# One value product per head from a sum of two masked matrices, and four adaLN sections of the second layer as row sums on VectorE

## The chip, the core and the metric

The kernel runs on one core of a Trainium2 chip. Its engines work in parallel, each through its own queue of instructions in order: PE (TensorE, matrix products), DVE (VectorE, elementwise work), ACT (ScalarE, activations and copies), POOL (GpSimd, here memsets and a few small loads) and SP (SyncE, which issues nearly all loads). The metric is the device time of one execution in microseconds (us), lower is better.

## What is computed

The reference is a two-layer transformer block. There are 256 latent and 256 context tokens of width 1024. Each layer has modulated RMSNorm, one input projection, three parallel head groups (A: differential attention, B: windowed attention, C: bidirectional gated linear attention), an output projection and a feed-forward part: a dense SwiGLU of width 2816 in the first layer, a top-2 of 8 experts SwiGLU of width 3584 in the second. Cut to the two places that the change touches:

```python
for layer in range(DEPTH):
    mod_l = (silu_c @ ada_w[layer] + ada_b[layer])[:, None, :]      # 6 sections of 1024
    mod_c = (silu_cc @ ada_w[layer] + ada_b[layer])[None, None, :]
    sh1_l, sc1_l, g1_l, sh2_l, sc2_l, g2_l = jnp.split(mod_l, 6, axis=-1)
    ...
    h_l = rms_norm(xl, norm1_g[layer]) * (1.0 + sc1_l) + sh1_l

# group C, forward and again on the flipped sequence, the two results added
att = jnp.where(causal, jnp.einsum('nbhcd,nbhsd->nbhcs', q_dec, k_inv), 0.0)
o_intra = jnp.einsum('nbhcs,nbhse->nbhce', att, vc)
```

The adaLN product has only two rows, the SiLU of the condition of the latent tokens and that of the context tokens, against a matrix of 1024 x 6144 per layer (25 MB in fp32). Everything is fp32; large products are made of three passes over high and low parts of the operands (hhi, hlo, whi, wlo).

## The kernel before

The whole kernel is planned before it is written: `add` registers each operation with its engine, an estimated time, what it waits for, a rank and the rings (buffers in rotation) that it takes and gives back. A list scheduler then starts, on each engine, the ready operation of lowest rank, and the instructions go out in that order. So a change of one operation can reorder others around it.

In time the stages of the profiled execution are: start and input projections of the first layer to about 190 us, its attention to 340, the dense FFN from about 352 to 715, the second layer's norm, projection and mixing (latent tokens only as queries) to about 950, and the experts to the end.

**The adaLN product.** `ada` makes `nb` blocks of 128 columns of one layer. It loads the columns of `ada_w` in two halves of four 128-row blocks through SP's queue, into a ring of large buffers. For each half it issues four products, L442, in which the two condition rows (padded to 32) are the small operand and the weights stream through as `nb * 128` columns; each product has its own 32 output columns of the array. ACT copies the result (L219, tile adar), PE transposes it (L452, tile adat), and DVE adds the four partial rows and the bias (L456, L457). In the FFN, `fill` is a list of such calls that `ffn` hands out, two after each chunk: two blocks of three for the last sections of the first layer, and then blocks 0 to 31 of the second layer, which are its first four sections, as ten calls of three blocks and one of two. The second layer's other two sections come later, in its mixing.

**The dense FFN.** Two halves of 1408 columns, each in chunks of at most 512. For each chunk the weights come in 1 MB loads; ACT makes the high part (whi, L219) and DVE the low part (wlo, L385); PE runs the three passes L645, L646 and L647 over 512 tokens. ACT takes the SiLU of the gate (fsg, L1651), DVE multiplies (L1658) and forms fhl.

**Group C.** `outC` makes one tile of 128 tokens (two chunks of 64) with four heads. For each head PE forms the products of keys and queries for both directions (paC, L1070); DVE copies those that the mask admits into one of two buffers of two 128x128 matrices, which hold zeros elsewhere (att, L1078); PE then multiplies each of the two matrices with the same values and adds both into poC (L1074). The first layer has 4 such tiles, the second 2, so 24 heads in all.

Of the kernel before, what the change touches and what calls it, by code (L numbers as in the profile page):

```python
# [11 lines left out]
F32 = mybir.dt.float32  # L12
# [10 lines left out]
KD = 8  # L23
# [9 lines left out]
def _const_arrays():  # L33
# [55 lines left out]
class Plan:  # L89
# [83 lines left out]
def trunk(ctx: ExitStack, tc: tile.TileContext, A, out, dbg=None):  # L173
# [101 lines left out]
            between()  # L275
        newton()

    plan = Plan(big=2, sm=4, hi=2, lo=2, raw=2, sp=2, work=10, long=24, mixC=2, b16=2, units=5, oC=2)
    add = plan.add


# [184 lines left out]
        return have  # L466

    mod = {}

    def amul(l, sec, g, nm):  # L470

# [186 lines left out]
    wmaskb = pc.tile([128, 2, 128], BF)  # L658
    bonesT = C("bones")
    att_bufs = []  # L660
    for i in range(2):
# [146 lines left out]

    wg, wu, wd = A["ffn_w_gate"][0], A["ffn_w_up"][0], A["ffn_w_down"][0]
    FILL = 5000  # L810
    EARLY = 32

    def mixing(l, base, t, tiles, wC, started=None):

# [235 lines left out]
        def outC(i, have, rank):  # L1050
            w = {}
            prev = None
            for pr in range(2):
# [9 lines left out]
                for hh in range(2):  # L1063
                    h = 2 * pr + hh

                    def products_(pr=pr, hh=hh, h=h):
                        r = slice(64 * hh, 64 * hh + 48)
                        w["pa", h] = P1((128, 2, 128), nm="paC")
                        for dr in range(2):
                            mm(w["pa", h][:, dr, :], G["ki", i, pr][r, dr, :], G["qd", i, pr][r, dr, :], start=True, stop=True)  # L1070

                    def values(hh=hh, h=h):
                        for dr in range(2):
                            mm(w["po"][:, 96 * h:96 * h + 96], att_bufs[hh][:, dr, :], T["vC", i][:, 96 * h:96 * h + 96],  # L1074
                               start=False, stop=hh == 1 and dr == 1)

                    a = add("PE", 0.44, products_, [x, *done["qk", i, pr]], rank, ["sm"])
                    a = add("DVE", 0.36, lambda hh=hh, h=h: nc.vector.copy_predicated(att_bufs[hh], mask, w["pa", h]),  # L1078
                            [a, turn.get(hh)], rank, (), ["sm"])
                    prev = turn[hh] = add("PE", 0.4, values, [a, prev, done["vC", i]], rank, (),  # L1080
                                          ["work"] + (["sp"] if pr == 1 else []) if hh == 1 else ())

            def copied_():
# [409 lines left out]
        for b in range(EARLY if last else 16, 48 if last else 42, 2):  # L1493
# [96 lines left out]
    def ffn(base, t, tiles, first_rank):  # L1590
# [3 lines left out]
                kk = 4 * hk + k  # L1594
                mm3(at(m), w.w[0][:, k, ms], w.w[1][:, k, ms], t["hi"][:, kk, :], t["lo"][:, kk, :], kk == 0, kk == KD - 1)

        fill = [(0, b, min(3, 48 - b)) for b in range(42, 48, 3)] + [(1, b, min(3, EARLY - b)) for b in range(0, EARLY, 3)]
        read = []
        sums = [[], []]
        silu = None  # L1600
        for g in range(2):
# [3 lines left out]
            for ci, (c0, cn) in enumerate(((0, 512), (512, 512), (1024, 384))):  # L1605
# [959 lines left out]
```

## Time and profile before

| | |
|---|---|
| three runs | 1921.57, 1925.91, 1927.15 us, median 1925.91 |
| the profiled execution | 1931.52 us, span in the trace 1929.7 us, mean granted clock of PE 0.99 |
| PE busy | 1880.7 us, 97% of the span |
| DVE busy | 1368.1 us, 71% |
| ACT busy | 1135.9 us, 59% |
| POOL busy | 38.9 us, 2% |
| moved by DMA | 474 MB, mean 246 GB/s |
| chain that ended last | PE 86%, DVE 6%, DMA 4%, ACT 3%; L442 of `ada` alone 2% |

The profile is one execution; its own time is the one against which a sum can be made, and it lies 5.6 us above the median of the three runs. The share of busy time is an average over stages, and a busy PE says little of how well it is fed, since the ends of matmuls are modelled; what a matmul costs is better read from the distance of two starts. In the rows below, a tile's name is the program's, an arrow points from inputs to output, and the bracket behind an instruction gives the idle time just before it and what ended it.

### The profile page before, as it was taken

How to read it: one execution, taken by the hardware profiler on the slowest of the kernel's cores; microseconds unless marked ns; L12 is line 12 of the kernel's file. 1: busy time of each engine (PE TensorE's matmuls, PEld its weight loads, DVE VectorE, ACT ScalarE, POOL GpSimd, SP SyncE). 2: the span in 40 equal slices, each digit the busy share in tenths (PEclk: the TensorE clock that was granted, in tenths of full speed). 3: DMA queues.
4: the chain of work that ended last, by engine and by line, in shares of the span. 5: the costliest groups of instructions: out<-in, count | busy, mean ns of one | idle time of the engine just before them, and what ended most of it. 6: DMA issues, size and time to landing. Idle time of an engine off the chain costs nothing.

```text
span 1929.7 us, 27430 instructions
## 1 busy us (share of the span) xinstructions
PE 1880.7 (97%) x10129; PEld 1511.6 (78%) x10129; DVE 1368.1 (71%) x2269; ACT 1135.9 (59%) x1906; POOL 38.9 (2%) x44
## 2 busy tenths in 40 slices
PE   7999999999999999999999999999999999999997
PEld 4888678877787799887888767888886688888765
DVE  5564887433333345758799786999988789999787
ACT  4443774323132325448677676777777777777676
POOL 1000200000000000011000000000000000000000
PEclk9999999999999999999999998999999999999999
DMA  9313532445434422347789898999999999999992
GB/s 295 109 55 101 183 105 82 139 135 185 164 120 137 153 74 88 93 141 245 258 316 359 343 374 341 368 362 381 355 352 368 397 360 360 380 366 363 356 366 104
DMA packets 178318, 474.38 MB, mean 246 GB/s; under 512 B 13193, under 2 KB 74337, under 8 KB 164481
## 3 DMA queue, kind: packets, MB, share of 16 engines
q1 hardware_dynamic: 177792, 472.37, 68.0%
q8 instruction: 82, 1.34, 0.3%
q0 software_dynamic: 384, 0.19, 0.1%
q14 instruction: 60, 0.48, 0.1%
HBM read 471.47 MB, written 1.05 MB: 245 GB/s over the span
## 4 chain that ended last, share of the span: by engine, by line
PE 86%; DVE 6%; DMA 4%; ACT 3%; issue 1%; SPq 0%; DVEq 0%; ACTq 0%
PE py L2311 12%; PE up L2229 12%; PE gate L2229 12%; PE acc L645 9%; PE acc L647 8%; PE acc L646 8%; DVE mlo L1885 2%; PE adap L442 2%; PE acc L855 2%; DMA idle<-in_ada_w 2%; PE acc L857 2%; PE acc L856 2%; PE py L2309 1%; PE pT L1241 1%; PE mtp L2288 1%; ACT mhi L219 1%
## 5 line engine op out<-in xcount | busy, mean ns | idle before, releaser
L1885 DVE TENSOR_TENSOR mlo<-early,mhi 128x1024 fp32r<-128x1024 f32 (+1 forms) x250 | 278.6, 1160 | 25.1 <-ACT mhi L219 23.5
L219 ACT ACTIVATE mhi<-early 128x1024 fp32r<-128x1024 f32 (+1 forms) x252 | 237.7, 996 | 43.7 <-PE py L2311 18.7
L385 DVE TENSOR_TENSOR wlo<-raw,whi 128x512 fp32r<-128x512 f32 (+4 forms) x292 | 150.4, 564 | 157.8 <-ACT whi L219 157.1
L219 ACT ACTIVATE whi<-raw 128x512 fp32r<-128x512 f32 (+4 forms) x292 | 134.9, 525 | 181.8 <-PE acc L646 147.0
L645 PE MATMUL acc<-hhi,whi 128*128 128x512 f32 (+1 forms) x576 | 217.4, 377 | 2.9 <-DVE rC L885 1.9
L1885 DVE TENSOR_TENSOR mlo<-more,mhi 128x1024 fp32r<-128x1024 f32 (+1 forms) x176 | 202.2, 1196 | 25.4 <-ACT mhi L219 23.5
L646 PE MATMUL acc<-hlo,whi 128*128 128x512 f32 (+1 forms) x576 | 210.6, 366 | 2.4 <-DVE hlo L579 2.4
L647 PE MATMUL acc<-hhi,wlo 128*128 128x512 f32 (+1 forms) x576 | 210.6, 366 | 0.5 <-DVE wlo L385 0.5
L2311 PE MATMUL py<-mhi,hid 128*128 128x512 f32 x696 | 193.7, 405 | 6.9 <-ACT mhi L219 3.7
L219 ACT ACTIVATE mhi<-more 128x1024 fp32r<-128x1024 f32 (+1 forms) x176 | 171.8, 1031 | 26.6 <-PE up L2229 12.9
L2311 PEld LDWEIGHTS py<-mhi,hid 128*128 128x128 f32 x696 | 131.5, 192 | 42.6 <-ACT mhi L219 9.7
L1885 DVE TENSOR_TENSOR mlo<-mraw,mhi 128x1024 fp32r<-128x1024 f32 (+1 forms) x116 | 134.5, 1202 | 16.6 <-ACT mhi L219 16.5
L1885 DVE TENSOR_TENSOR mlo<-spare,mhi 128x1024 fp32r<-128x1024 f32 (+1 forms) x114 | 129.7, 1183 | 10.8 <-ACT mhi L219 10.6
L645 PEld LDWEIGHTS acc<-hhi,whi 128*128 128x128 f32 x576 | 108.7, 189 | 35.2 <-issue 11.2
L2311 PE MATMUL py<-mlo,hid 128*128 128x512 f32 x416 | 122.4, 407 | 2.5 <-DVE mlo L1885 2.5
L219 ACT ACTIVATE mhi<-mraw 128x1024 fp32r<-128x1024 f32 (+1 forms) x116 | 114.2, 1036 | 18.1 <-PE py L2311 9.2
L646 PEld LDWEIGHTS acc<-hlo,whi 128*128 128x128 f32 x576 | 108.9, 189 | 19.2 <-DVE hlo L579 3.4
L647 PEld LDWEIGHTS acc<-hhi,wlo 128*128 128x128 f32 x576 | 108.7, 189 | 18.7 <-DVE wlo L385 0.9
L219 ACT ACTIVATE mhi<-spare 128x1024 fp32r<-128x1024 f32 (+1 forms) x114 | 110.2, 1020 | 14.4 <-PE py L2311 9.6
L2311 PEld LDWEIGHTS py<-mlo,hid 128*128 128x128 f32 x416 | 79.3, 193 | 26.7 <-DVE mlo L1885 11.0
L2229 PE MATMUL gate<-mlo,xh 128*128 128x512 f32 x280 | 78.4, 402 | 0.0
L2229 PE MATMUL gate<-mhi,xh 128*128 128x512 f32 x280 | 76.0, 394 | 0.0
(443 smaller groups left out, 3693.3 us busy)
## 6 DMA issues: line engine op xcount, KB each, us to landing
early<-in_moe_w_gate SPq DMA_DIRECT2D x42, 1024.0 KB, 7.4
early<-in_moe_w_down SPq DMA_DIRECT2D x41, 1024.0 KB, 6.5
more<-in_moe_w_gate SPq DMA_DIRECT2D x38, 1024.0 KB, 7.0
early<-in_moe_w_up SPq DMA_DIRECT2D x37, 1024.0 KB, 7.0
mraw<-in_moe_w_up SPq DMA_DIRECT2D x25, 1024.0 KB, 6.6
spare<-in_moe_w_down SPq DMA_DIRECT2D x25, 1024.0 KB, 6.8
more<-in_moe_w_up SPq DMA_DIRECT2D x25, 1024.0 KB, 7.3
more<-in_moe_w_down SPq DMA_DIRECT2D x25, 1024.0 KB, 5.7
```

Of the source, the lines that this page charges most:

```text
L219: act(o, i, AF.Copy)
L385: tt(l_, v, h, op=OP.subtract)
L442: mm(w["pm"][32 * g:32 * g + 32, :n], sil[:, 4 * i + g, :], w["raw"][4 * i + g], start=i == 0, stop=i == 1, tile_position=(0, 32 * g))
L645: mm(o, lh, rh, start=start, stop=False)
L646: mm(o, lh, rl, start=False, stop=False)
L647: mm(o, ll, rh, start=False, stop=stop)
L855: mm(p, t["hi"][:, kk, s], w.w[0][:, k, :], start=kk == 0, stop=False)
L856: mm(p, t["hi"][:, kk, s], w.w[1][:, k, :], start=False, stop=False)
L857: mm(p, t["lo"][:, kk, s], w.w[0][:, k, :], start=False, stop=kk == KD - 1)
L1885: tt(l, w, h, op=OP.subtract)
L2229: mm(outs[q], x[a](kk), w[b][:, j, :], start=i + kk == 0, stop=i == len(x) and kk == KD - 1)
L2311: mm(outs[q], v[a][:, kk % 4, :], w[b][:, j, :], start=first and i + kk == 0, stop=i == len(v) and kk + 1 == nk)
```

## The change

Two things are changed.

In group C, DVE adds the two masked 128x128 matrices of a head (atts, one more TENSOR_TENSOR behind each L1078), and PE multiplies the sum with the values: one product instead of two.

The second layer's sections 0 to 3 are taken out of `fill`. A new function `ada_rows` makes each of them in two halves of 512 columns. The weights of a half come as eight loads of 128x512 (256 KB) on the Pool queue, into a ring of three buffers (adw). DVE multiplies each with the two conditions, one value per partition, and sums up: per half 2 TENSOR_SCALAR and 14 SCALAR_TENSOR_TENSOR of 128x512. Then, for each condition, DVE transposes 32x32 blocks and reduces (2 of each per half). One PE product per section with a constant 128x128 matrix (`four`) adds the four groups of 32 rows and lays the sum out, and DVE adds the bias in four small pieces. So there are 64 loads, 16 TENSOR_SCALAR, 112 SCALAR_TENSOR_TENSOR, 16 transposes, 16 reductions, 4 products and 16 small additions. All of it but the last two steps has the rank `base + 9000`, behind the FFN's own work. The bytes of `ada_w` are the same as before; 22 loads of SP's queue are gone. The constant adds 64 KB to an early load.

```diff
+    c["four"] = p[:, None] % 32 == p[None, :] % 32
...
+    def ada_rows(l, sec, rank, after):
...
+        for j in range(2):
+            c0 = sec * 1024 + j * 512
+            for k in range(KD):
+                def load(k=k, c0=c0):
+                    w["w"] = k2.tile([128, 1, 512], F32, name="adw", tag="adw", bufs=3)
+                    w[k] = w["w"]
+                    nc.gpsimd.dma_start(out=w[k], in_=A["ada_w"][l, k * 128:k * 128 + 128, c0:c0 + 512].rearrange("(k p) f -> p k f", p=128))
+
+                after = [add("PoolDMA", 0.75, load, after, rank, ["adw"])]
+                for i in range(1):
+                    for v in range(2):
+                        def summed(k=k, i=i, v=v):
...
+                            o, x, s = w["acc"][:, v], w[k][:, i], sil[:, k + i, v:v + 1]
+                            if k + i == 0:
+                                ts(o, x, s, None, op0=OP.mult)
+                            else:
+                                stt(o, x, s, o, op0=OP.mult, op1=OP.add)
...
+            for v in range(2):
+                def grouped(v=v, j=j):
...
+                    nc.vector.transpose(t, w["acc"][:, v])
+                    nc.vector.tensor_reduce(w["r"][:, v, 4 * j:4 * j + 4].rearrange("p m q -> p (m q)"),
+                                            t.rearrange("p (b i) -> p b i", i=32), axis=AX.X, op=OP.add)
...
+        def over_groups():
+            w["p"] = P1((128, 2, 8, 4), nm="adap")
+            mm(w["p"].rearrange("p v m q -> p (v m q)"), C("four"), w["r"].rearrange("p v m q -> p (v m q)"), start=True, stop=True)
...
-    EARLY = 32
+    ROWS = 4
...
+                    def masked(hh=hh, h=h):
+                        nc.vector.copy_predicated(att_bufs[hh], mask, w["pa", h])
+                        tt(att_sums[hh], att_bufs[hh][:, 0, :], att_bufs[hh][:, 1, :], op=OP.add)
+
                     def values(hh=hh, h=h):
-                        for dr in range(2):
-                            mm(w["po"][:, 96 * h:96 * h + 96], att_bufs[hh][:, dr, :], T["vC", i][:, 96 * h:96 * h + 96],
-                               start=False, stop=hh == 1 and dr == 1)
+                        mm(w["po"][:, 96 * h:96 * h + 96], att_sums[hh], T["vC", i][:, 96 * h:96 * h + 96], start=False, stop=hh == 1)
...
-        fill = [(0, b, min(3, 48 - b)) for b in range(42, 48, 3)] + [(1, b, min(3, EARLY - b)) for b in range(0, EARLY, 3)]
+        fill = [(0, b, min(3, 48 - b)) for b in range(42, 48, 3)]
...
+                if rows_ is None:
+                    rows_ = read[:1]
+                    for sec in range(ROWS):
+                        rows_ = ada_rows(1, sec, base + 9000 + sec, rows_)
```

On PE, in the FFN, one removed block of `ada` stands between the three passes of the FFN like this (before):

```order
L647 MATMUL acc_4366<-hhi,wlo 128x512
L442 MATMUL adap<-idle,sil 32x384 x4
L645 MATMUL acc<-hhi,whi 128x512
...
L647 MATMUL acc<-hhi,wlo 128x512
L442 MATMUL adap<-idle,sil 32x384 x4
L645 MATMUL acc_4366<-hhi,whi 128x512
...
L647 MATMUL acc_4366<-hhi,wlo 128x512
L452 MATMUL adat<-cst,adar 128x128 x3
L645 MATMUL acc_4366<-hhi,whi 128x512
```

After, PE has for a whole section this one product there (the passes' lines are 59 higher):

```order
L706 MATMUL acc<-hhi,wlo 128x512
L515 MATMUL adap<-adsum,cst_80 128x64
L704 MATMUL acc_4301<-hhi,whi 128x512
L705 MATMUL acc_4301<-hlo,whi 128x512
L706 MATMUL acc_4301<-hhi,wlo 128x512
```

The three matmuls that were between the parts of a block now follow each other without them.

On DVE, at the FFN's start, the low parts of the first weights and the first products stand like this (before):

```order
L385 TENSOR_TENSOR wlo<-raw,whi 128x512 x12
L1658 TENSOR_TENSOR fsg<-fsg,acc 128x512
L385 TENSOR_TENSOR fhl<-fsg,fhh 128x512
L1658 TENSOR_TENSOR fsg<-fsg,acc 128x512
L385 TENSOR_TENSOR fhl<-fsg,fhh 128x512
```

And after:

```order
L386 TENSOR_TENSOR wlo<-raw,whi 128x512 x8
L496 TENSOR_SCALAR adacc<-adw,sil 128x512 x2
L498 SCALAR_TENSOR_TENSOR adacc<-adw,sil,adacc 128x512 x9
L386 TENSOR_TENSOR wlo<-raw,whi 128x512 x4
L1720 TENSOR_TENSOR fsg<-fsg,acc 128x512
L498 SCALAR_TENSOR_TENSOR adacc<-adw,sil,adacc 128x512
L386 TENSOR_TENSOR fhl<-fsg,fhh 128x512
L1720 TENSOR_TENSOR fsg<-fsg,acc 128x512
```

Eleven of the new sums, which use five and a half loads, stand ahead of the low parts of the next weights, and single ones between the FFN's own operations.

On PE, in group C of the second layer, the products with the values (poC from vC) and their neighbours stand like this before, where att_95 and att_97 are the two buffers:

```order
L1074 MATMUL poC<-vC_6926,att_95 128x96 x2
L1074 MATMUL poC<-vC_6926,att_97 128x96 x2
L1058 MATMUL poC<-spC,qkC 128x192 x2
L1070 MATMUL paC<-qkC 128x128 x4
L645 MATMUL acc_7150<-hhi,whi 128x256
```

And after, where atts_95 and atts_96 are the sums:

```order
L1137 MATMUL poC<-vC_7038,atts_95 128x96
L1130 MATMUL paC<-qkC 128x128 x2
L1137 MATMUL poC<-vC_7038,atts_96 128x96
L1118 MATMUL poC<-spC,qkC 128x192 x2
L1130 MATMUL paC<-qkC 128x128 x2
L704 MATMUL acc_7262<-hhi,whi 128x256
```

Each head has one product with the values instead of two, and the key-query products of the next heads have come apart around them.

## Rows read from the trace of the kernel before

**Rows 1.** Windows: a stretch, its length, busy us per engine, clock, DMA
```profile
core 0: us, PE busy (x) PEld busy (x) DVE busy (x) ACT busy (x) POOL busy (x), PEclk, DMA share, GB/s
358.00:615.00 257.00, 256.16 (x1216) 197.30 (x1216) 82.83 (x159) 71.83 (x134) 0.00 (x0) 1.00 0.46 152
...
1100.00:1500.00 400.00, 394.08 (x1770) 313.36 (x1769) 344.73 (x338) 295.22 (x349) 0.00 (x0) 0.99 0.96 364
```

**Rows 2.** Timeline of PE in the FFN without `ada`: start, us, instruction, twelve passes apart
```profile
423.33 0.39 PE L647 MATMUL acc<-hhi,wlo 128*128 128x512 f32 x1
...
426.05 0.39 PE L647 MATMUL acc<-hhi,wlo 128*128 128x512 f32 x1
```

**Rows 3.** Timeline of PE around one block whose halves stand apart
```profile
480.13 0.39 PE L647 MATMUL acc<-fhh,wlo 128*128 128x512 f32 x1
480.45 0.85 PE L442 MATMUL adap<-idle,sil 128*32 128x384 f32 x8
...
483.87 0.39 PE L647 MATMUL acc<-fhh,wlo 128*128 128x512 f32 x1
...
487.60 0.39 PE L647 MATMUL acc<-fhh,wlo 128*128 128x512 f32 x1
487.83 0.49 PE L452 MATMUL adat<-cst,adar 128*128 128x128 f32 x3
...
490.70 0.39 PE L647 MATMUL acc<-fhh,wlo 128*128 128x512 f32 x1
```

**Rows 4.** Timeline of PE around a block whose halves stand together
```profile
498.86 0.39 PE L647 MATMUL acc<-fhh,wlo 128*128 128x512 f32 x1
499.18 1.50 PE L442 MATMUL adap<-idle,sil 128*32 128x384 f32 x16
...
503.27 0.39 PE L647 MATMUL acc<-fhh,wlo 128*128 128x512 f32 x1
```

**Rows 5.** Waits of PE in the FFN, 360 to 720: total us, times, longest
```profile
PE acc L645 <- ACT fsg L1651: 0.7, 2, 0.4
```

**Rows 6.** Timeline of PE, group C of the first layer: the products with the values
```profile
106.72 1.11 PE L1074 MATMUL poC<-vC,att 128*128 128x96 f32 x8
107.67 0.52 PE L1058 MATMUL poC<-spC,qkC 128*128 128x192 f32 x2
```

**Rows 7.** Group C of the second layer: timelines of DVE and PE, and the window
```profile
804.08 0.77 DVE L1078 COPY_PREDICATED att<-cst,paC 128x256 f32<-128x256 uint32 x2
...
804.58 1.13 PE L1074 MATMUL poC<-vC,att 128*128 128x96 f32 x8 [0.44 <-DVE att L1078]
...
801.00:816.00 15.00, 14.56 (x114) 12.49 (x113) 9.43 (x28) 4.35 (x13) 0.00 (x0) 1.00 0.39 124
```

**Rows 8.** DVE by line and shape: count, busy us, mean ns, idle before
```profile
L1281 DVE SCALAR_TENSOR_TENSOR unit<-unit,rcA 128x512 f32<-128x512 f32 x16 | 12.1, 755 | 0.2
L1323 DVE TENSOR_SCALAR unit<-unit,smx 128x512 f32<-128x512 f32 x24 | 10.8, 482 | 0.1
...
L385 DVE TENSOR_TENSOR wlo<-raw,whi 128x128 fp32r<-128x128 f32 x16 | 4.6, 285 | 0.0
L1236 DVE TENSOR_REDUCE mx<-sB 128x2 f32<-128x512 f32 x6 | 4.1, 688 | 1.2 <-PE sB L1221 1.0
```

**Rows 9.** Timeline of DVE at the FFN's start
```profile
354.19 4.91 DVE L385 TENSOR_TENSOR wlo<-raw,whi 128x512 fp32r<-128x512 f32 x8 [9.23 <-ACT whi L219]
367.72 2.50 DVE L385 TENSOR_TENSOR wlo<-raw,whi 128x512 fp32r<-128x512 f32 x4 [8.62 <-ACT whi L219]
```

**Rows 10.** Tile lp (64 KB, Pool queue): ns of issuing, then landing
```profile
L672 POOL DMA_DIRECT2D lp<-in_a_lambda x2: 573/626/680, 18.2 to 151.4; - x2
...
DMA to landing us min/median/max: 3.2/4.3/5.4
```

**Rows 11.** Tile idle (`ada`'s loads through SP's queue, 256 KB and more): landing
```profile
DMA to landing us min/median/max: 3.9/6.3/9.9
```

**Rows 12.** Waits of SP's queue from 900 on: total us, times, longest
```profile
SPq L1839 <- DVE mlo L1885: 654.3, 272, 9.1
```

More of the change, by code (lines that the diff above doesn't have):

```diff
@@ L276, in rsqrt @@
         newton()
-    plan = Plan(big=2, sm=4, hi=2, lo=2, raw=2, sp=2, work=10, long=24, mixC=2, b16=2, units=5, oC=2)
+    plan = Plan(big=2, sm=4, hi=2, lo=2, raw=2, sp=2, work=10, long=24, mixC=2, b16=2, units=5, oC=2, adw=3, adacc=1)
     add = plan.add
@@ L468, in trunk, with places, biased @@
     mod = {}
+    def ada_rows(l, sec, rank, after):
+        w = {}
+        def places():
+            w["r"] = k2.tile([128, 2, 8, 4], F32, name="adsum", tag="adsum", bufs=2)
+        last = None
+        for j in range(2):
[9 more added lines that the diff above has]
+                        def summed(k=k, i=i, v=v):
+                            if k + i + v == 0:
+                                w["acc"] = k2.tile([128, 2, 512], F32, name="adacc", tag="adacc", bufs=1)
+                            o, x, s = w["acc"][:, v], w[k][:, i], sil[:, k + i, v:v + 1]
[3 more added lines that the diff above has]
+                                stt(o, x, s, o, op0=OP.mult, op1=OP.add)
+                        last = add("DVE", 0.85, summed, [*after, last, have_c], rank, ["adacc"] if k + i + v == 0 else (),
+                                   ["adw"] if v else ())
+            for v in range(2):
+                def grouped(v=v, j=j):
+                    if "r" not in w:
+                        places()
+                    t = K2(nm="adt")
+                    nc.vector.transpose(t, w["acc"][:, v])
+                    nc.vector.tensor_reduce(w["r"][:, v, 4 * j:4 * j + 4].rearrange("p m q -> p (m q)"),
+                                            t.rearrange("p (b i) -> p b i", i=32), axis=AX.X, op=OP.add)
+                last = add("DVE", 1.6, grouped, [last], rank, ["work"], ["work"] + ["adacc"] * v)
+        def over_groups():
+            w["p"] = P1((128, 2, 8, 4), nm="adap")
+            mm(w["p"].rearrange("p v m q -> p (v m q)"), C("four"), w["r"].rearrange("p v m q -> p (v m q)"), start=True, stop=True)
+        def biased():
+            for q in range(4):
+                r = slice(32 * q, 32 * q + 32)
+                tt(mods[l][r, sec * 8:sec * 8 + 8, :], w["p"][r, :, :, q].rearrange("p v m -> p m v"),
+                   adab[l][r, sec * 8:sec * 8 + 8, None].to_broadcast([32, 8, 2]), op=OP.add)
+        a = add("PE", 0.25, over_groups, [last], 55, ["sm"])
+        a = add("DVE", 0.7, biased, [a, have_small], 55, (), ["sm"])
+        for b in range(sec * 8, sec * 8 + 8):
+            mod[l, b] = a
+        return after
@@ L660, in trunk @@
     att_bufs = []
+    att_sums = [pc.tile([128, 128], F32, name=f"atts{i}") for i in range(2)]
     for i in range(2):
@@ L1070, in products_ @@
                             mm(w["pa", h][:, dr, :], G["ki", i, pr][r, dr, :], G["qd", i, pr][r, dr, :], start=True, stop=True)
+                    def masked(hh=hh, h=h):
+                        nc.vector.copy_predicated(att_bufs[hh], mask, w["pa", h])
+                        tt(att_sums[hh], att_bufs[hh][:, 0, :], att_bufs[hh][:, 1, :], op=OP.add)
                     def values(hh=hh, h=h):
-                        for dr in range(2):
-                            mm(w["po"][:, 96 * h:96 * h + 96], att_bufs[hh][:, dr, :], T["vC", i][:, 96 * h:96 * h + 96],
-                               start=False, stop=hh == 1 and dr == 1)
+                        mm(w["po"][:, 96 * h:96 * h + 96], att_sums[hh], T["vC", i][:, 96 * h:96 * h + 96], start=False, stop=hh == 1)
                     a = add("PE", 0.44, products_, [x, *done["qk", i, pr]], rank, ["sm"])
-                    a = add("DVE", 0.36, lambda hh=hh, h=h: nc.vector.copy_predicated(att_bufs[hh], mask, w["pa", h]),
-                            [a, turn.get(hh)], rank, (), ["sm"])
-                    prev = turn[hh] = add("PE", 0.4, values, [a, prev, done["vC", i]], rank, (),
+                    a = add("DVE", 0.58, masked, [a, turn.get(hh)], rank, (), ["sm"])
+                    prev = turn[hh] = add("PE", 0.2, values, [a, prev, done["vC", i]], rank, (),
                                           ["work"] + (["sp"] if pr == 1 else []) if hh == 1 else ())
@@ L1492, in mixing @@
             finA(tq, R + 10 * (nA // 2 * (tq + 1) + 4))
-        for b in range(EARLY if last else 16, 48 if last else 42, 2):
+        for b in range(ROWS * 8 if last else 16, 48 if last else 42, 2):
             ada(l, b, 2, ["raw"], base + FILL + b, [wB[1].loaded])
@@ L1595, in chunk_product @@
                 mm3(at(m), w.w[0][:, k, ms], w.w[1][:, k, ms], t["hi"][:, kk, :], t["lo"][:, kk, :], kk == 0, kk == KD - 1)
-        fill = [(0, b, min(3, 48 - b)) for b in range(42, 48, 3)] + [(1, b, min(3, EARLY - b)) for b in range(0, EARLY, 3)]
+        fill = [(0, b, min(3, 48 - b)) for b in range(42, 48, 3)]
+        rows_ = None
         read = []
```

## The prediction

> **What bounds the kernel now.** I read the windows first, cut by stage, to see whether the stage that the change touches is paced by PE. In the FFN, PE is busy 256.16 of 257 us at a granted clock of 1.00, while DVE is busy 82.83 us, POOL not at all, and the DMA engines 46% [rows 1]. So there an instruction taken from PE is time taken from the kernel, and DVE has 174 us to give. Among PE's waits in the FFN the largest entry is 0.7 us, twice, for ACT [rows 5]: nothing else is late. Next I read PE's timeline for what an instruction costs. Between two starts twelve passes apart lie 2.72 us [rows 2], 0.227 us each, although the profile gives each 0.39 us of duration. I count costs by such distances, since durations overlap. Last come the experts, where a gain in the FFN could be lost again: DMA is at 96% and 364 GB/s, but PE is busy 394.08 of 400 us [rows 1], and SP's queue, which issues the loads, waits 272 times, 654.3 us, for DVE to have read a buffer [rows 12]. The loads follow the compute there, so the whole stage should move forward with its start.
>
> **Taken off PE in the FFN.** Eleven blocks go: ten of 384 columns and one of 256. In one whose halves stand apart, the stretch from 480.13 to 483.87 holds twelve passes and the first four products: 3.74 us, less 2.72 for the passes, is 1.02 us. The second half, to 487.60, gives 3.73 less 2.72, 1.01 us, and the transposes, to 490.70, 3.10 less 2.72, 0.38 us [rows 3]. Together 2.41 us. Eight of the ten blocks read like this: 19.3 us. In the other two the halves stand together, and 498.86 to 503.27 is 4.41 less 2.72, 1.69 us [rows 4]; with the transposes' 0.38 that is 2.07 each, 4.1 us. The block of 256 columns I estimate at two thirds of that, 1.4 us. Sum: **24.8 us** less. The two waits for ACT may go with the blocks behind which they stand, at most 0.7 us more [rows 5]; I count nothing. The ACT copies and small DVE sums of these blocks lie on engines that have time left.
>
> **Added to PE in the FFN.** Four products of 64 columns with the constant matrix. No row shows one. From below, a transpose of 128 columns costs 0.38/3 = 0.13 us; from above, four products of 384 columns 1.02 us [rows 3]. The ends are 0.5 and 4.1 us for four. In size they are nearest to the transposes, but each sits alone between other matrices; I take 0.3 each, **1.2 us** more.
>
> **Group C.** Four value products of two heads cost the 0.95 us from 106.72 to 107.67 [rows 6], 0.475 a head; half of them gone is 0.24 a head. In the first layer, where other products stand beside them and PE is full, I count all 16 heads: **3.8 us** less. In the second layer PE already waits 0.44 us for the masked copy before its value products, and is busy 14.56 of 15 us [rows 7]. There the new addition, 0.285 us by the nearest row [rows 8], lengthens what PE waits for by more than the 0.24 saved. For 8 heads I take **0**, between 1.9 us less (8 x 0.24, addition hidden) and 2.3 us more (8 x 0.285, nothing saved). In the first layer the same exposure could eat half, 1.9 us. Group C lies between 5.7 us less and 0.4 us more. The extra 64 KB of constants are loaded ahead of their use; I count nothing.
>
> **Added to DVE, and what hides it.** A half section is 2 TENSOR_SCALAR of 0.482, 14 SCALAR_TENSOR_TENSOR of 0.755 and two pairs of transpose and reduction. A reduction of this size is 0.688 us [rows 8]; no row has such a transpose, and I give it the same, between a half and twice that. That is 0.96 + 10.57 + 2.75 = 14.3 us, eight times **114 us**, with both conditions included (103 to 125 with the transposes' ends). In the FFN window, eight of the eleven removed blocks (18.6 us) leave about 238 us, of which DVE's own work keeps 82.8: 156 us are free, 41 more than needed. So on average it hides. But DVE works in the order written, and the sums stand ahead of low parts (wlo) that PE needs. At the FFN's start, eleven sums, five and a half loads, stand between wlo x8, which ends at 359.1, and the next wlo x4, at 367.72 [rows 9]. Three loads fit the buffers early, so three are there. The fourth is issued when the first buffer has been read, about 360.1, and with a landing of L us the eleven end near 363.9 + L.
>
> **The loads.** What is L for 256 KB on the Pool queue? The only row has 64 KB: issuing 0.63 us, landing 3.2 to 5.4 us, the longer one in the busy start [rows 10]. Through SP's queue such weights land in 3.9 to 9.9 us, median 6.3, most of them in that busy start too [rows 11]. In the FFN the DMA engines are half idle, so I take L = 4.2, between 3.2 and 9.9. The eleven sums then end at 368.1, 0.4 us behind the old start of wlo. Afterwards a load comes round every (L + 1.5)/3 us, 1.9 at L = 4.2 (three buffers, two sums of 0.75), against 238/64 = 3.7 us that there are: nothing is late on average up to L = 9.6. A burst of five sums' loads between two groups of low parts, which PE uses up in 48 x 0.227 = 10.9 us, takes 5 x (L + 1.5)/3 us, and fits to L = 5.0. Beyond it DVE falls behind within a burst, by 5 us at L = 8; since weights are prepared a tile ahead, PE feels little of one such burst and more of several in a row. At L = 4.2 I count **0**. POOL itself has nothing else to do there [rows 1], and the queue behind the last load holds only the second layer's memsets. SP's queue loses 22 loads and gains nothing.
>
> One rule speaks against this way of loading. Row first: the two lp loads were issued in 0.57 to 0.68 us [rows 10]. The Trainium skill, "SBUF — State Buffer", section "Who interferes with whom", says that a DMA issued by GpSimd needs GpSimd to write its descriptors, and that it cannot while VectorE is in a mode that uses both ports, into which a tensor_scalar can fall, but not an operation with two inputs. Here this would touch 16 of the 128 sums; if each held up a load by its own 0.482 us and none of it were hidden, the sum would be 7.7 us worse. No row so far shows a load against such an operation, and I count nothing.
>
> **Sum.** -24.8 + 1.2 - 3.8 + 0 = **-27.4 us**. Against the profiled execution's own 1931.5 us that is 1904.1. That execution is 5.6 us above the median of the runs, 1925.9, which I take as the base: **1898.5 us**. With the bounds: -24.8 - 0.7 + 0.5 - 5.7 = -30.7, and from the lowest run, 1921.6, that is 1890.9; on the other side -24.8 + 4.1 + 0.4 = -20.3, from the highest run, 1927.2, 1906.9.
>
> **Rivals.**
> *Sums late in bursts.* The Pool loads land in 7 to 9.6 us. DVE then falls behind by some 5 us in bursts, and PE waits for wlo or for DVE's product in two to four places: 10 to 20 us of the gain are lost, about 1908 to 1919. For it: SP's own loads have such times [rows 11], and the 64 KB rows carry a quarter of the bytes. Against: DMA at 46%.
> *Given back later.* The experts' stage is then set by its loads, at 96% of DMA time, and starts no earlier than these allow; the gain shrinks to some 0 to 6 us, 1920 to 1926. Against: SP waits for DVE there, not for transfers [rows 12], and PE is full.
> *Slower: the loads are the bound.* If a load needs more than 9.6 us, the 64 loads outlast the FFN, and since sums stand ahead of low parts, PE is drawn out with them. From (238 + 27)/64 = 4.1 us per load, L = 10.9, the gain is used up; at L = 12 the loads take 64 x 4.5 = 288 us, 50 more than there is, and the kernel ends at 1898.5 + 50, about 1949. For it: 9.9 us is the longest landing in SP's rows [rows 11], and each Pool load waits for a buffer that DVE must free. Against: that was the busy start, and the same bytes were moved in the FFN before.
>
> **How the numbers follow.** The forecast, 1891 to 1907 around 1898.5, gets 0.68; sums late in bursts 0.14; given back later 0.09; slower 0.09. What a measurement of this kernel can tell from no change is about 0.3%, 5.8 us. So faster 0.82, same 0.09, slower 0.09. The range goes from 1890 to 1918: it holds the forecast and nearly all of the late bursts, and leaves out the last two cases, 0.18.
>
> **What would show it.** Right: in the changed kernel's FFN, PE's window is about 24 us shorter and still over 99% busy; DVE rises by about 114 us; adw loads land in 3 to 6 us; PE has no new wait for wlo or fsg; the experts' stage is as long as before, moved forward; group C of the first layer is 3 to 4 us shorter, of the second unchanged. Wrong: waits of PE for wlo of several us behind runs of SCALAR_TENSOR_TENSOR (late sums), DVE waiting for adw all along (loads the bound), sums much longer than 0.755 us, or an experts' stage longer than before.

## The result, and the profile after

The changed kernel takes 1894.92 us (median of four runs, 1894.37 to 1896.79) against 1925.88 us. The ratio is 0.9843, with a 95% interval from 0.983 to 0.9855: 31 us less, where 27.4 were forecast (1898.5 us). A second set of runs, further down, gave 0.9848 (0.9834 to 0.9862).

The two traces are best read by stage, cut at the same instruction in both: the first product of group C, the first product of the dense FFN, its last one, and the first gather of the experts. Windows with a stage's length, then busy us of PE, PEld, DVE, ACT, POOL, the granted clock, DMA share and GB/s; before:

```profile
0.00:91.50 91.50, 77.85 (x480) 59.66 (x481) 48.05 (x141) 39.24 (x97) 6.50 (x18) 0.98 0.67 213
91.50:330.80 239.30, 235.53 (x1665) 190.03 (x1663) 170.60 (x502) 130.05 (x367) 17.73 (x15) 1.00 0.36 106
330.80:727.60 396.80, 395.06 (x2079) 317.26 (x2080) 147.52 (x300) 120.56 (x236) 0.00 (x0) 1.00 0.41 135
727.60:945.80 218.20, 212.33 (x1594) 182.28 (x1592) 154.31 (x433) 124.47 (x325) 14.68 (x11) 1.00 0.48 157
945.80:1919.70 973.90, 959.14 (x4311) 761.84 (x4312) 843.95 (x887) 720.37 (x881) 0.00 (x0) 0.99 0.93 350
```

and after:

```profile
0.00:92.20 92.20, 76.50 (x480) 58.28 (x481) 47.69 (x141) 39.24 (x97) 6.48 (x18) 0.98 0.68 213
92.20:328.20 236.00, 232.26 (x1633) 186.36 (x1631) 175.21 (x518) 130.31 (x367) 19.30 (x18) 1.00 0.37 111
328.20:699.90 371.70, 370.69 (x1880) 312.82 (x1881) 247.21 (x454) 115.14 (x225) 32.73 (x61) 1.00 0.43 142
699.90:917.40 217.50, 211.42 (x1578) 181.56 (x1576) 157.04 (x440) 124.64 (x325) 14.68 (x11) 1.00 0.48 157
917.40:1882.60 965.20, 950.13 (x4311) 753.73 (x4312) 843.85 (x887) 720.45 (x881) 0.00 (x0) 1.00 0.93 353
```

Stage by stage the change is +0.7, -3.3, -25.1, -0.7 and -8.7 us. In the FFN, PE has 199 instructions fewer and is as full as before, and DVE has 99.7 us more, where the prediction said about 114; 4.6 us of the difference are the removed blocks' own small sums (DVE 147.52 us before, 142.88 in the kernel further down that has neither form). But the last stage also lost 8.7 us, with the same instructions of PE, DVE and ACT to the last one, and nothing of the change lies in it. Its 4311 products kept PE busy 959.14 us before and 950.13 after: what differs there is the clock. One stretch of it before, and after a stretch that begins with the same work, 35 us earlier:

```profile
1160.00:1190.00 30.00, 28.60 (x110) 21.47 (x109) 20.42 (x21) 17.33 (x24) 0.00 (x0) 0.83 0.91 350
```
```profile
1125.00:1155.00 30.00, 27.91 (x135) 20.30 (x134) 21.58 (x23) 19.32 (x26) 0.00 (x0) 1.00 1.00 386
```

At a mean of 0.83, a third of the 30 us ran at the lower level of 1.2 GHz. It begins behind a wait of PE that stands in both executions, before and after:

```profile
1170.03 2.02 PE L2311 MATMUL py<-mhi,hid 128*128 128x512 f32 x4 [1.40 <-DVE hid L2296]
```
```profile
1135.36 1.20 PE L2377 MATMUL py<-mhi,hid 128*128 128x512 f32 x4 [1.40 <-DVE hid L2362]
```

After the same 1.40 us of idle time the clock fell in one execution and not in the other. In this stage of the execution of before it fell four times (near 950, 1075, 1175 and 1800), in that of after twice (near 1400, and near 1760, the same place as the last of before). Windows of 5 us put, by their mean clock, some 27 us at the lower level before and some 7 after; the 20 us between them are an estimated 10 us of work, near the 9.0 by which PE's busy time differs. The two profiled executions are 37 us apart for this reason, the medians 31. The experiments show below how much of the 31 us is work.

The rows that answer to [rows 8], DVE by line and shape, with count, busy us, mean ns and idle before:

```profile
L498 DVE SCALAR_TENSOR_TENSOR adacc<-adw,sil,adacc 128x512 f32<-128x512 f32 x112 | 78.5, 746 | 15.6 <-DMA adw<-in_ada_w 15.5
L507 DVE STREAM_TRANSPOSE adt<-adacc 128x512 f32<-128x512 f32 x16 | 11.3, 704 | 0.0
L508 DVE TENSOR_REDUCE adsum<-adt 128x16 f32<-128x512 f32 x16 | 11.0, 686 | 0.6
L1134 DVE TENSOR_TENSOR atts<-att 128x128 f32<-128x128 f32 x24 | 7.0, 292 | 1.4 <-PE poC L1137 0.6
L496 DVE TENSOR_SCALAR adacc<-adw,sil 128x512 f32<-128x512 f32 x16 | 7.0, 480 | 0.0
```

The sums have the durations of their nearest rows (746 against 755 ns, 480 against 482), and the transpose, for which there was no row, 704 against the 688 given to it. Together the row sums (without atts) are 107.8 us busy; 114 were worked out from single durations, which overlap a little in a run of equal instructions.

The tile adw, which answers to [rows 10] and [rows 11]: the issues on POOL, who waited, and the time from issue to landing:

```profile
L486 POOL DMA_DIRECT2D adw<-in_ada_w x64: 536/536/575, 246.2 to 578.1; - x64
...
  DVE adacc L498: 15.5, 7
...
DMA to landing us min/median/max: 2.9/3.5/7.6
```

A load lands in 3.5 us (4.2 were taken), and DVE waits for one only 7 times, 15.5 us in all, in its spare time. Where the longest one falls can be seen on DVE's timeline at the FFN's start, which answers to [rows 9]:

```profile
351.59 4.91 DVE L386 TENSOR_TENSOR wlo<-raw,whi 128x512 fp32r<-128x512 f32 x8 [9.23 <-ACT whi L220]
...
357.21 2.73 DVE L498 SCALAR_TENSOR_TENSOR adacc<-adw,sil,adacc 128x512 f32<-128x512 f32 x4
365.00 3.40 DVE L498 SCALAR_TENSOR_TENSOR adacc<-adw,sil,adacc 128x512 f32<-128x512 f32 x5 [5.05 <-DMA adw<-in_ada_w]
368.31 2.49 DVE L386 TENSOR_TENSOR wlo<-raw,whi 128x512 fp32r<-128x512 f32 x4
```

Three loads are there, the fourth is issued at 357.59 and lands at 365.00, beside two loads of FFN weights of 1 MB that SP issued at 355.92. So the low parts wlo come at 40.1 us after the FFN's first product, where they came at 36.9 before, 3.2 us later. PE does not feel it. Its waits from 340 to 720 (total us, times, longest), which answer to [rows 5]; the two for wlo stand with the same figures in the trace of before:

```profile
PE acc L706 <- DVE wlo L386: 0.8, 2, 0.5
PE acc L705 <- DVE hlo L638: 0.7, 3, 0.3
PE acc L704 <- ACT whi L220: 0.2, 1, 0.2
```

The product with the constant, on PE's timeline between the passes:

```profile
412.56 0.39 PE L706 MATMUL acc<-hhi,wlo 128*128 128x512 f32 x1
412.79 0.33 PE L515 MATMUL adap<-adsum,cst 128*128 128x64 f32 x2
...
413.48 0.39 PE L706 MATMUL acc<-hhi,wlo 128*128 128x512 f32 x1
```

Three passes and the product take 0.92 us; less 3 x 0.227 for the passes, the product costs 0.24 us (0.3 were taken).

### The profile page after: what moved, and what is told of

Its sections match the earlier page's. It is cut to its first block, busy times and chain, and to the rows that moved or that the text cites. A ratio compares the mean times of both kernels' runs of the same rounds, so it can differ in the third digit from the quotient of the medians.

```text
span 1892.6 us, 27209 instructions
## 1 busy us (share of the span) xinstructions
PE 1841.8 (97%) x9881; PEld 1493.3 (79%) x9881; DVE 1474.7 (78%) x2447; ACT 1131.0 (60%) x1895; POOL 73.2 (4%) x108
## 5 line engine op out<-in xcount | busy, mean ns | idle before, releaser
L1951 DVE TENSOR_TENSOR mlo<-more,mhi 128x1024 fp32r<-128x1024 f32 (+1 forms) x176 | 202.2, 1196 | 24.9 <-ACT mhi L220 23.6
L220 ACT ACTIVATE mhi<-more 128x1024 fp32r<-128x1024 f32 (+1 forms) x176 | 171.8, 1031 | 26.6 <-PE up L2295 12.8
L1951 DVE TENSOR_TENSOR mlo<-mraw,mhi 128x1024 fp32r<-128x1024 f32 (+1 forms) x116 | 134.5, 1202 | 16.6 <-ACT mhi L220 16.5
L498 DVE SCALAR_TENSOR_TENSOR adacc<-adw,sil,adacc 128x512 f32<-128x512 f32 x112 | 78.5, 746 | 15.6 <-DMA adw<-in_ada_w 15.5
```

What stands on the lines that cost most here:

```text
L220: act(o, i, AF.Copy)
L498: stt(o, x, s, o, op0=OP.mult, op1=OP.add)
L1951: tt(l, w, h, op=OP.subtract)
```

## Experiments

Twelve kernels were run, the changed kernel itself once more among them, in three sets of four, each set on one chip beside the kernel before. Where a few us matter, runs are compared at the same granted clock, for a reason that the last experiment shows.

### Group C alone

The masked sums and the single value product, in the kernel before:

```diff
-                        for dr in range(2):
-                            mm(w["po"][:, 96 * h:96 * h + 96], att_bufs[hh][:, dr, :], T["vC", i][:, 96 * h:96 * h + 96],
-                               start=False, stop=hh == 1 and dr == 1)
+                        mm(w["po"][:, 96 * h:96 * h + 96], att_sums[hh], T["vC", i][:, 96 * h:96 * h + 96], start=False, stop=hh == 1)
```

> The kernel before with group C's part of the change alone (two masked matrices added, one value product per head; the adaLN fill as before). Theory: 16 heads of the first layer save 0.24 us each on a full PE and the second layer's 8 nothing, so 3.8 us less, about 1922; in the trace the second half of layer 1's projections is 3 to 4 us shorter and layer 2's mixing unchanged. Rival, the addition is exposed on the way from the masked copy to the product: nothing gained, 1925 to 1928.

Measured: 1921.52 us (11 runs) against 1925.05, ratio 0.9978 (0.9969 to 0.9987). In its trace the stretch from group C's first product to the FFN is 236.1 us, against 239.3 before and 236.0 in the changed kernel; the FFN is 396.8 as before, and the second layer up to the experts 218.0 against 218.2. The theory holds, at 3.2 us for the first layer instead of 3.8. Part of what is missing can be seen on PE's timeline of the changed kernel, next to [rows 6]:

```profile
107.44 0.46 PE L1137 MATMUL poC<-vC,atts 128*128 128x96 f32 x2
...
108.12 0.46 PE L1137 MATMUL poC<-vC,atts 128*128 128x96 f32 x2 [0.22 <-DVE atts L1134]
108.42 0.52 PE L1118 MATMUL poC<-spC,qkC 128*128 128x192 f32 x2
```

Where two heads' value products come close behind their masked copies, PE now waits 0.22 us for the addition. This happens once in the first layer's group C.

### The row sums alone

The changed kernel with group C as before.

> The kernel before with the four sections as row sums alone (group C as before). Theory: 24.8 us of PE less, 1.2 more, about 23.6 less than before, 1902; the first matmul of the experts comes 23 to 25 us earlier. Rival, the changed kernel gained more than the sum because the FFN gained more: then this alone is 27 us or more faster, 1899 or less. If instead the extra lies in the experts' clock, the times of this kernel scatter with the granted clock and the start of the experts moves by 24 us all the same.

Measured: 1900.8 us (4 runs), ratio 0.9882 (0.9867 to 0.9897). Its FFN is 371.7 us, the same as in the changed kernel, and the experts start 25.3 us earlier than before, 0.3 more than the 23 to 25 expected. The two parts alone are -3.9 and -25.3 us up to the experts, -28.4 together. Their sum is 0.8 us more than both together, and the start ahead of group C alone differs by 1.2 us between these traces (91.0 to 92.2). So no help or hindrance between the two parts can be seen.

### No product for the four sections

```diff
-        fill = [(0, b, min(3, 48 - b)) for b in range(42, 48, 3)] + [(1, b, min(3, EARLY - b)) for b in range(0, EARLY, 3)]
+        fill = [(0, b, min(3, 48 - b)) for b in range(42, 48, 3)]
...
+    nc.gpsimd.memset(mods[1][:, :32, :], 0.0)
```

> The kernel before without any product for the second layer's sections 0 to 3 (left out: these four sections are zero, so the tokens' values and routes behind them differ), group C as before. It shows what the removed blocks cost and, against the kernel with row sums alone, what the row sums cost. Theory: 24.8 us less than before, 1901, and 1.2 us under the kernel with row sums alone. Rival, the sums and loads are not hidden: 3 to 10 us under it. Only the time to the start of the experts is compared strictly, since routes differ behind it.

Measured: the FFN takes 370.7 us, 26.1 less than before; the row sums put 1.0 us of that back (1.2 were taken). The blocks of `ada` cost 26.1 us instead of 24.8. Of the 1.3 us between, 0.7 are PE's two waits for ACT behind such blocks [rows 5], which the prediction named as a bound and did not count; they are gone in the waits shown above; the other 0.6 stay open. The times (median 1897.48 of 5) depend on other routes behind it, and nothing is taken from them.

### The loads on SP's queue

```diff
-                    nc.gpsimd.dma_start(out=w[k], in_=A["ada_w"][l, k * 128:k * 128 + 128, c0:c0 + 512].rearrange("(k p) f -> p k f", p=128))
+                    nc.sync.dma_start(out=w[k], in_=A["ada_w"][l, k * 128:k * 128 + 128, c0:c0 + 512].rearrange("(k p) f -> p k f", p=128))
```

> The changed kernel with the 64 loads on SP's queue instead of Pool's. Theory A, only the loads' bytes count and the DMA engines are half idle: same time, 1895, within 2 us. Theory B, a load that waits on SP's queue for a buffer that VectorE must free holds the FFN's weight loads behind it, so weights come late and PE waits: 5 to 40 us slower, 1900 to 1935, with PE waiting for ACT's whi in the FFN. I lean to B.

Measured: 1894.77 us (5 runs), as with the Pool queue; the FFN is 371.7 us again. The theory to which I leaned is wrong. SP's waits from 340 to 720 and the landing of adw in this kernel:

```profile
SPq L698 <- DVE wlo L386: 151.8, 22, 23.5
...
SPq L486 <- DVE adacc L498: 59.5, 52, 3.1
SPq L486 <- DVE adacc L496: 17.7, 7, 3.4
SPq L486 <- DMA adw<-in_ada_w: 16.4, 7, 5.4
```
```profile
DMA to landing us min/median/max: 2.5/3.6/7.1
```

SP waits some 94 us with adw loads at its head, at most 5.4 us at once, while it stands 151.8 us with the FFN's weights, up to 23.5 us at once, until their buffers are read. The weights were waiting for buffers anyway, and the short waits ahead of them cost nothing: PE's waits are the three shown above, to the same tenth. Here the choice of the queue does not matter.

That the loads land alike from both queues also bears on the rule weighed in the prediction (the Trainium skill, "SBUF — State Buffer", section "Who interferes with whom"). None of the 64 issues on POOL took more than 575 ns, and SP's loads landed no faster: no run here shows the lock that the page describes. But a load is issued behind a sum that frees its buffer, so few of them can have fallen beside one of the 16 TENSOR_SCALAR; the rule itself is not tested.

### Two buffers, and one

```diff
-oC=2, adw=3, adacc=1)
+oC=2, adw=2, adacc=1)
...
-                    w["w"] = k2.tile([128, 1, 512], F32, name="adw", tag="adw", bufs=3)
+                    w["w"] = k2.tile([128, 1, 512], F32, name="adw", tag="adw", bufs=2)
```

> The changed kernel with two buffers for the weights of the row sums instead of three; the order of instructions is the same. By the prediction's formula with the measured landing of 3.5 us and issuing of 0.54, a load comes round every (3.5 + 0.5 + 1.5)/2 = 2.8 us instead of 1.8; five of a burst take 14 us against 10.9. Theory: VectorE falls some 3 us behind in bursts, and a tile's lead hides it: 0 to 4 us slower at the same clock, 1895 to 1899. Rival, bursts are what PE feels at once: 8 bursts by 3 us, about 1919.

> The changed kernel with one buffer; the planner spreads the sums over a somewhat longer stretch of the FFN. Each load then waits for the sums of the one before it: 3.5 + 0.5 + 1.5 = 5.5 us a load, 64 loads 352 us, against some 300 us in which the sums now stand. The rival of the prediction (loads are the bound, since sums stand ahead of low parts on VectorE) expects PE drawn out by some 50 us, about 1945. If PE only needs the sections late and VectorE's order does not matter, under 1900.

Measured: two buffers 1900.84 us (4 runs), some 6 us slower than three, and 4.5 to 5.4 at the same clock: a little past the theory's 4 and far from the rival. PE waited 2.6 us at one product with the constant and 2.4 us at the first layer's blocks, which neither had named, and the FFN was 380.4 us, 8.7 longer. One buffer took 1986.56 us (4 runs), 92 us slower, ratio 1.0316 (1.029 to 1.0342) to the kernel before, where about 1945 were expected. With one, the loads ran at (729.4 - 355.1)/62 = 6.0 us each, where 5.5 were worked out, and the FFN grew by 92.1 to 463.8 us at a clock of 0.92: PE idled 63.7 us more, and the same 1880 instructions were busy 28.4 us longer. The rival "the loads are the bound" is thus real, and it is the ring of buffers that keeps it away. PE's waits from 340 to 760 with one buffer show where it strikes:

```profile
PE adap L515 <- DVE adsum L508: 29.6, 4, 9.3
PE acc L706 <- DVE wlo L386: 25.7, 10, 5.4
PE adap L443 <- DMA idle<-in_ada_w: 8.7, 2, 4.8
```

Nearly half of the waiting is not for the low parts but at the four products with the constant: PE stands at a product whose sums are late, with all the passes of the FFN behind it. The prediction had priced these products by their size and had not named this wait.

### Each sum twice

```diff
                                 stt(o, x, s, o, op0=OP.mult, op1=OP.add)
+                                stt(o, x, sil[:, k + i, 2:3], o, op0=OP.mult, op1=OP.add)
```

> The changed kernel with each of the 112 three-operand sums followed by a second one that adds nothing (scalar zero): 112 x 0.745 = 83 us more on VectorE in the stretch 356 to 588, which has some 41 to 65 us free. Theory (the sums are hidden only as long as VectorE's total fits): VectorE becomes the bound there and PE waits for wlo and fsg, 20 to 45 us slower, 1915 to 1940. Rival, the sums slide behind the FFN and PE does not feel them: within 5 us of 1895.

Measured: 1932.63 us (10 runs), 38 us slower than the changed kernel: the cover is used up. The PE waits (340 to 760) and two windows of this kernel:

```profile
PE adap L516 <- DVE adsum L509: 22.5, 4, 7.7
```
```profile
460.00:500.00 40.00, 32.35 (x134) 26.35 (x133) 39.31 (x69) 7.84 (x14) 5.14 (x10) 0.87 0.48 158
500.00:540.00 40.00, 40.00 (x178) 33.13 (x177) 39.32 (x64) 9.73 (x18) 5.05 (x10) 1.00 0.43 139
```

DVE is busy 39.3 of 40 us. PE stands 22.5 us at the four products; the expectation had named wlo and fsg, and for wlo PE waits only 1.8 us. Where it has stood for 7.7 us the clock falls: in the first window it is busy 32.35 of 40 us at 0.87, in the next, full again, at 1.00. The whole FFN took 409.5 us, with 27.6 idle and a mean clock of 0.96. Of the 37.8 us that it grew, 26.6 are idle time and 11.2 the same 1880 instructions at the lower clock: idle time of PE costs more than itself.

### Each sum twice, the products later

```diff
-        a = add("PE", 0.25, over_groups, [last], 55, ["sm"])
+        a = add("PE", 0.25, over_groups, [add("none", 40.0, lambda: None, [last])], 55, ["sm"])
```

> The kernel with doubled sums, but each section's product with the constant matrix stands about 40 us (180 passes) later on PE. With doubled sums PE waited 22.5 us at these four products for VectorE, and its clock fell behind each wait. Theory A (VectorE's total is the bound, the product only the place where PE meets it): the wait moves to the low parts wlo, and the time stays within 8 us of 1932.6. Theory B (the product's early place is the cost): most of the 38 us comes back, 1895 to 1905. VectorE was busy 39 of 40 us in that stretch, so I lean to A, with the last 8 us as its slack.

Measured: 1916.04 us (4 runs), between the two theories: 16.6 of the 38 us come back. The FFN is 395.3 us, and PE now waits like this:

```profile
PE acc L707 <- DVE wlo L386: 11.0, 12, 2.6
PE adap L443 <- DMA idle<-in_ada_w: 3.5, 1, 3.5
```

Both reasons were there. Nearly half of the loss was where the product stood, with long waits and the clock that they cost (0.96 before, 0.99 now); the rest is DVE's total, which PE meets at wlo in twelve short waits, and for 5.3 us at the first layer's blocks of `ada` (3.5 for a load, 1.8 for DVE).

### Two buffers, the products later

The same edit with `adw=2`.

> The kernel with two buffers, its four products about 40 us later on PE. With two buffers PE waited 2.6 us at one product, the clock fell behind it, and the FFN was 8.7 us longer in the trace. Theory (only the product felt the late sums, weights kept their lead): the FFN comes back to 371 to 373 us and the time to 1894 to 1897. Rival, VectorE's lateness reaches PE through wlo: 1899 or more.

Measured: 1899.35 us (5 runs), the FFN 378.0 us instead of 380.4 with two buffers and 371.7 with three; the theory had 371 to 373. So the product's place explains only a part here. There is no wait at the product any more and none for wlo beyond the old 0.8 us; the rest came by a way that neither theory named. PE's timeline of this kernel at the first layer's two remaining blocks, and then SP's issues:

```profile
381.89 0.85 PE L443 MATMUL adap<-idle,sil 128*32 128x384 f32 x8 [1.76 <-DMA idle<-in_ada_w]
...
395.24 1.26 PE L443 MATMUL adap<-idle,sil 128*32 128x384 f32 x8 [2.73 <-DMA idle<-in_ada_w]
```
```profile
387.31 0.37 SPq L698 DMA_DIRECT2D raw<-in_ffn_w_up  x1
387.77 2.00 SPq L432 DMA_DIRECT2D idle<-in_ada_w  x2
```

and SP's in the changed kernel:

```profile
381.75 0.37 SPq L698 DMA_DIRECT2D raw<-in_ffn_w_up  x1
382.21 3.68 SPq L432 DMA_DIRECT2D idle<-in_ada_w  x2
```

DVE's late low parts free the weights' buffer 5.6 us later (6.4 counted from the FFN's start), SP's next weight load waits for it, and the loads for `ada` stand behind that load in SP's queue. These blocks have no such lead as the FFN's weights, so PE waits 4.5 us for them, and the clock falls to 0.96 in that stretch.

### All six sections as row sums

```diff
-    ROWS = 4
+    ROWS = 6
```

> The changed kernel with the second layer's sections 4 and 5 as row sums too, in place of eight blocks of 256 columns in the second layer's mixing. Theory: 8 x 1.4 us of PE less, 0.6 more, and the 57 us of VectorE's sums lie in the end of the FFN and the start of the second layer: about 11 us faster, 1884. Rival, VectorE is needed there (norms, splits of weights) and PE waits for it: half or all of it lost, 1890 to 1900.

Measured: 1900.37 us (4 runs), 5.5 us slower than with four, although 8 blocks of `ada` fewer stand on PE. The FFN is 373.7 us, 2.0 longer, with 1.1 us more of waits for wlo. The second layer up to the experts grows from 217.5 to 220.3; the other kernels' traces lie between 217.4 and 219.0. A window of it in this kernel, and the same place in the changed kernel:

```profile
881.00:901.00 20.00, 15.66 (x135) 13.59 (x134) 11.70 (x34) 9.70 (x25) 0.00 (x0) 0.91 0.60 200
```
```profile
880.00:900.00 20.00, 20.00 (x193) 19.22 (x189) 15.78 (x42) 11.72 (x30) 0.00 (x0) 1.00 0.77 215
```

In the second layer up to the experts PE is busy 6.8 us less than in the changed kernel and idle 9.5 us more: what was taken off came back as waits, among others 3.0 us for whi and 1.4 each for oCl (from DVE) and a unit (from ACT). So the rival was right in size, at the end of its range, and wrong in its reason: in this window DVE is not busier (11.70 of 20 us). The longest of these waits lies in it, on ACT and then on PE:

```profile
892.09 1.15 ACT L220 ACTIVATE wh<-raw 128x512 fp32r<-128x512 f32 x2 [3.25 <-DMA raw<-in_w_out]
```
```profile
893.97 0.58 PE L704 MATMUL acc<-mBh,whi 128*128 128x256 f32 x1 [2.98 <-ACT whi L220]
```

ACT stands 3.25 us for a load of the output projection's weights, and the high parts that PE needs come behind it in ACT's order. In the changed kernel ACT waits 3.03 us for such a load too, but these high parts stand ahead of it, and PE does not wait. So a third of the new waiting comes from another order of the plan. For the rest, that PE follows a chain of ACT and DVE in the mixing and that the blocks of `ada` filled its gaps fits the waits for oCl and the unit; no run separates the two.

### The first layer's last section too, and the changed kernel again

```diff
-        for b in range(ROWS * 8 if last else 16, 48 if last else 42, 2):
+        for b in range(ROWS * 8 if last else 16, 48 if last else 40, 2):
...
-        fill = [(0, b, min(3, 48 - b)) for b in range(42, 48, 3)]
+        fill = []
...
-                    for sec in range(ROWS):
-                        rows_ = ada_rows(1, sec, base + 9000 + sec, rows_)
+                    for i, (l, sec) in enumerate([(0, 5), (1, 0), (1, 1), (1, 2), (1, 3)]):
+                        rows_ = ada_rows(l, sec, base + 9000 + i, rows_)
```

> The changed kernel with the first layer's last section (5) as row sums too, ahead of the other four: the FFN's last two blocks and one of the first layer's mixing go, 16 loads and 28.6 us on VectorE come. Theory: 2 x 2.4 us of PE less in the FFN, 0.3 more, up to 1.4 less in the mixing, and VectorE has the time: 4 to 6 us faster than the changed kernel run beside it. Rival, VectorE (busy 31 of 40 us now, some 35 then) falls behind within bursts and PE waits at a product or for wlo: no gain or slower.

> The changed kernel itself, beside the three others and the kernel before on one chip. If the 31 us of the first comparison were 28.4 us of work and the rest the clock that these few executions happened to get, then at equal granted clock (0.995) it is 28 to 29 us under the kernel before, and the medians differ by 27 to 31. If the change itself keeps the clock up in the experts, its executions lie at a higher clock than those of the kernel before: medians of clock 0.995 to 0.996 against 0.994.

Measured: 1890.18 us with the fifth section (5 runs, ratio 0.9831 to the kernel before, 0.9814 to 0.9847) against 1894.63 for the changed kernel beside it (5 runs). At a clock of 0.995 it is 1889.9 (2 runs) against 1894.7 (3 runs of both sets), 4.8 us faster, as expected. Its FFN:

```profile
327.30:694.90 367.60, 366.32 (x1843) 312.22 (x1844) 272.32 (x494) 113.95 (x221) 41.45 (x77) 1.00 0.44 144
```

It is 4.1 us shorter, PE is as full, and DVE has 25 us more. Its second layer up to the experts takes 218.7 us, though, and the experts start only 3.8 and 2.6 us earlier than in the changed kernel's two traces. This version beats both kernels, and it also takes away the two blocks whose loads were the weak place in the last experiment but one.

Medians over all sets, by the granted clock of the run (in brackets the number of runs):

| clock | kernel before | changed kernel | difference |
|---|---|---|---|
| 0.994 | 1925.1 (11) | 1896.4 (4) | -28.7 |
| 0.995 | 1923.6 (10) | 1894.7 (3) | -28.9 |
| 0.996 | 1921.9 (6) | 1893.6 (2) | -28.3 |

At the same clock the change is worth 28.3 to 28.9 us, and the traces up to the experts say 28.4. A thousandth of clock is 1 to 2 us. The median clock of the kernel before is 0.994 (39 runs), that of the changed kernel 0.995 (9 runs); this fits the rest of the 31 us, but does not show it. Whether the change itself keeps the clock up a little, or nine runs happened to have it, stays open: the five runs of the second set have a median of 0.994, and so have the runs with group C alone and with the row sums alone.

## Why the prediction was right

- **The bound.** PE in the FFN was the bound, and time taken from it came back whole: 25.1 us for 23.6 worked out, 26.1 less and 1.0 more. The method of counting by the distance of starts, less the passes between, missed 1.3 us of 26, of which the two waits for ACT are 0.7. This miss and that of group C, 0.6 the other way, partly cancel in the total.
- **Group C.** 3.2 us for 3.8 in the first layer. In the second layer the traces with this part and the blocks of sections 4 and 5 lie between 217.4 and 219.0 us from the FFN to the experts; the kernel before and that with the row sums alone, which have the old form, lie at 218.2 and 218.5. No gain or loss can be told from this scatter, for 0.
- **DVE's cover.** 107.8 us of sums for 114, and the cover was real: where they stand, 356.4 to 588, DVE was busy 180.44 of 231.6 us. The price past its end was also near: 83 us more, against some 41 free, gave 38 us, though part of that was the place of the products.
- **The loads.** 3.5 us for 4.2, so the formula for a round was safe by a factor of two with three buffers. The first eleven sums ended 16.8 us after the start of the low parts ahead of them, where 13.9 were worked out. The formula held; its term L was too small there, because the fourth load met the first weights and took 7.4 us. PE's lead hid it.
- **Given back later.** It was not: the experts' stage, at 93% of DMA time, started 28.4 us earlier and was no longer than before. SP's waits for buffers [rows 12] were the right row for this.
- **What was missed.** The size of the total was under by 3.6 us: 1.0 in the work, and the rest probably in the clock, which the sum took as given. And the rival of late sums named wlo as the place where PE would wait. With late sums it waits first at the products with the constant, and at blocks of `ada` whose loads stand behind weight loads on SP's queue. Neither wait arises with three buffers, so the number did not suffer, but the reason was incomplete: a small product that closes a long chain on another engine is a wait in PE's order, whatever its size.

## What to carry to other kernels

A product with two useful rows is cheap to move off TensorE where TensorE is the bound and VectorE has idle time that a sum over the stage shows; the same move cost time in the second layer's mixing, where TensorE waits for other engines and the freed time came back as waits. Count the ring of buffers as part of the price, since a round of loads is landing, issue and use divided by the buffers: here three were enough, two cost 5 to 6 us and one 92. Place the instruction that closes the moved chain well behind the planned end of that chain, because the engine that reaches it early stands there with everything behind it, and on TensorE the idle time also cost clock here (0.87 over 40 us around a wait of 7.7 us).

## What was not expected of the hardware

- The granted clock is the largest part of the scatter: between 0.991 and 0.997 the kernel before took 1930.6 to 1919.8 us. In the profiled execution of before it fell four times in the experts, in that of after twice: behind the same wait of 1.40 us it fell to the lower level in the one and stayed up in the other. What decides this, no run here shows.
- Loads of 256 KB landed alike from the Pool queue (2.9, 3.5 and 7.6 us) and from SP's (2.5, 3.6 and 7.1), and issuing took POOL 0.54 us each, next to a DVE that was busy four fifths of the time.
- The longest landing in the changed kernel, over 7 us where the median is 3.5, was met right beside the first 1 MB loads of the FFN's weights, at a mean DMA share of 43% over the FFN. The share of a stage says little of the one moment at which a load is due.
